# Fourth unit of the second MLP's down-projection in seven block products, and a later place for the last norm's transposes

## Chip, cores and metric

The kernel runs on one core of one Trainium2 chip. The metric is the device time of one execution in microseconds (us); for the kernel before, the median of three runs is 1207.76 us (1206.56 to 1208.12).

## What is computed

The reference is a trunk of two decoder layers on 512 tokens of width 1024, all in float32. Layer 0 mixes tokens by sliding-window attention beside a short convolution, layer 1 by gated linear attention. Each layer then has a gated MLP with a width-3 convolution, and a gated per-layer embedding. What the change touches is the end of layer 1:

```python
def _conv_ffn(h, w_up, conv_w, conv_b, w_down):
    u = _causal_depthwise_conv(h @ w_up, conv_w) + conv_b
    gate, up = jnp.split(u, 2, axis=-1)
    return (jax.nn.gelu(gate, approximate=False) * up) @ w_down      # w_down: 2816 x 1024
...
x = x + _conv_ffn(...)
gate = jax.nn.sigmoid(_rms_norm(x, norm) @ w_gate)                    # w_gate: 1024 x 1024
x = x + gate * (p_i @ w_proj)                                         # w_proj: 256 x 1024
```

## The kernel before, in words

**Layout.** The residual x is kept transposed as eight tiles `xT[m]` of 128 features x 512 tokens. A float32 product is made of three matmuls in a rounded type: each operand is split into a high part (a rounded copy, made by ScalarE) and a low part (the rest, a subtraction on VectorE), and the matmuls are high x high, high x low and low x high (`mm3`, lines 162 to 164; `cut` at 142 and 143 splits weights; `split` at 109 and 110 splits activations).

**Down-projection (`down`, from line 1088).** The 2816 rows of the weight are 22 blocks of 128, in three groups: B (0 to 7), A (8 to 13) and C (14 to 21). The 1024 output features are four *units* of 256, so a unit fills two PSUM banks. `plan` lists the steps in the order in which TensorE takes them: unit, row group, first and last block of the group, and as a fifth entry the unit whose block products are woven into this step. Inside `down` TensorE's order is written out by hand (`manual_schedule` at 1188); the other engines are ordered by a scheduler, which prefers what comes earlier in the program. Two such stages run, one per layer.

**Seven block products (`seven`, from line 857).** Group C of a unit is 8 row blocks x 256 features x 512 tokens. Taken as 2 x 2 blocks (even and odd row blocks, left and right features, left and right tokens) it is computed by seven products in place of eight. Each product is four row pairs x three matmuls, 256 tokens wide (lines 872 to 874). It needs sums and differences of weight blocks (`first_forms`, `more_forms`, `cut_blocks`, lines 811 to 855) and of activation blocks (`split_blocks`, 1006). The activation forms (`down_forms`) are made once per stage and lie in tiles with the tag b in the second MLP. In the first MLP all four units are computed this way; in the second MLP units 0, 1 and 2 are, and unit 3's group C is taken in two plain steps of four row blocks (`(3,"C",0,4)`, `(3,"C",4,8)`).

**After a unit.** `add` (line 1181) adds a unit's two banks to `xT`. Once `block_left` is 0, `finish` is called for the units that are complete. In the second MLP `finish` is `blocks` (line 287): gain, split, sums and differences for the block products of the next stage, and a square that is added up in the tile `self.acc` (line 285). Its scratch halves come from `both` (tag zt, two buffers), as do the weights that `load_inner` brings (line 1132); its results lie in tiles with the tags b (features 0 to 3) and a (4 to 7). The low and high parts of the activations of group B lie in tiles with tag a until their last use.

**Last stage (`ple1`, from line 1323).** The gate of layer 1, also by block products, with the weight as the moving operand. From line 1432 on TensorE, VectorE and ScalarE all take their instructions in program order. `add(X, "e1", ...)` is 24 matmuls into two banks X; the first two of eight steps of "s1" follow (six matmuls); then `end_norm` (line 322) transposes `self.acc` on TensorE (line 329), sums it on VectorE (331) and takes the root on GpSimd (172), which gives `self.r`. Then come two copies `ka` of X (line 1442), the split of `wt2` (line 1443), `load_p` (1444: eight transposes of p at line 1275 and their splits), the other six steps of "s1", and "s2" with `wt2` into X (line 1452). `self.r` is first read at line 1463. These are the lines on which the buffers of this place hang:

```python
self.acc = self.sp.tile([P, S], F32, tag="acc", name=self.nm("acc"), bufs=1)                      # 261
...
ka = [self.sp.tile([P, S], F32, tag="acc", name=self.nm("keep"), bufs=1), self.sq()]              # 1440
for k, x in zip(ka, X):
    nc.scalar.copy(k, x)
```

A tile whose tag has one buffer is written only once the instructions that use the earlier tile of that tag are done.

Of the kernel before, what the change touches and what calls it, by code (L numbers as in the profile page):

```python
# [56 lines left out]
class Kernel:  # L57
# [1030 lines left out]
    def down(self, i, acts, forms, both, work, finish):  # L1088


        nc, tc = self.nc, self.tc
        H = S // 2
        wd = self.a["ffn_w_down"][i].rearrange("(k p) n -> p k n", p=P)
        rows = {"A": (8, 14), "B": (0, 8), "C": (14, 22)}

        plan = [(0, "B", 0, 4), (0, "B", 4, 8), (0, "A", 0, 3), (0, "A", 3, 6)]
        plan += [(1, "A", 0, 3), (1, "A", 3, 6), (1, "B", 0, 4), (1, "B", 4, 8, 0)]
        plan += [(2, "B", 0, 4, 1), (2, "B", 4, 8, 2)]
        if i == 0:
            plan += [(2, "A", 0, 4, 3), (2, "A", 4, 6), (3, "B", 0, 4), (3, "B", 4, 8), (3, "A", 0, 3), (3, "A", 3, 6)]  # L1100
            loads = ["B0", "A0", "A1", "B1", "C0", "B2", "C2", "A2", "B3", "A3"]
            inner = ["C1", "C3"]
        else:
            plan += [(2, "A", 0, 3), (2, "A", 3, 6), (3, "B", 0, 4), (3, "B", 4, 8)]
            plan += [(3, "C", 0, 4), (3, "C", 4, 8), (3, "A", 0, 3), (3, "A", 3, 6)]
            loads = ["B0", "A0", "A1", "B1", "C0", "B2", "C2", "A2", "B3", "C3", "A3"]
            inner = ["C1"]
        blocked = 4 - i
        plan = [p if len(p) == 5 else p + (None,) for p in plan]
        got, cuts, gens, pending = {}, {}, {}, []  # L1110

        def pend():
            while pending:
                pending.pop(0)()

        def cols(u):
            return slice(2 * P * u, 2 * P * u + 2 * P)

        def load(key):
            k0, k1 = rows[key[0]]  # L1120
            u = int(key[1])
            raw = self.raw(k1 - k0, 2 * P)
            nc.sync.dma_start(raw, wd[:, k0:k1, cols(u)])
            got[key] = (raw, None)

        def load_inner(key):
            k0, k1 = rows[key[0]]
            u = int(key[1])
            parts = []
            for q in range(2):  # L1130
                t = both().rearrange("p a (b n) -> p (a b) n", n=2 * P)
                nc.sync.dma_start(t, wd[:, k0 + q : k1 : 2, cols(u)])
                parts.append(t)
            got[key] = (None, parts)

        def cut(t):
            u, name, k0, k1, _ = plan[t]
            cuts[t] = self.cut(got[f"{name}{u}"][0][:, k0:k1], "a")
            if k1 == rows[name][1] - rows[name][0] and loads:
                load(loads.pop(0))  # L1140

        def first_forms(u):
            raw, parts = got[f"C{u}"]
            ev, od = parts or self.by_parity(raw)
            gens[u] = ev, od, self.first_forms(ev, od, raw)

        def more_forms(u):
            ev, od, plain = gens[u]
            t13 = self.cut_blocks(ev)

            def rest():
                gens[u] = self.seven(od, (plain, t13, self.more_forms(ev, od)), acts[14:], forms, False)

            pending.append(rest)

        def cut_done(u):

            raw, _ = got[f"C{u}"]
            if raw is not None and loads:
                load(loads.pop(0))  # L1160
            elif raw is None and inner:
                load_inner(inner.pop(0))

        todo = []
        for t, p in enumerate(plan):
            todo.append((1, lambda t=t: cut(t)))
            if p[4] is not None:
                todo.append((1, lambda u=p[4]: first_forms(u)))
                todo.append((1, lambda u=p[4]: more_forms(u)))
        free = 3  # L1170

        def pump(n):
            nonlocal free
            free += n
            while todo and todo[0][0] <= free:
                need, f = todo.pop(0)
                free -= need
                f()

        def add(m, ps):  # L1180
            nc.vector.tensor_tensor(self.xT[m], self.xT[m], ps, ALU.add)

        due = [2 if u < blocked else 1 for u in range(4)]
        block_left = blocked
        next_unit = 0

        banks = {}
        with tc.manual_schedule(engines={ET.PE}):
            with tc.high_priority(offset=300):
                for _ in range(2):  # L1190
                    load(loads.pop(0))
                pump(0)
            for t, (u, name, k0, k1, s) in enumerate(plan):
                own = u not in banks
                if own:
                    banks[u] = [self.ps(), self.ps()]
                ends = t + 1 == len(plan) or plan[t + 1][0] != u
                joined = i == 0 and u == 3

                def steps(lo, hi):  # L1200
                    for k in range(lo, hi):
                        for c in range(2):
                            self.mm3(
                                banks[u][c], cuts[t](k, c * P, (c + 1) * P), acts[rows[name][0] + k0 + k],
                                start=own and k == 0, stop=ends and k == k1 - k0 - 1, skip_group_check=joined,
                            )

                def settled(ends):
                    nonlocal next_unit
                    if ends:  # L1210
                        for c in range(2):
                            add(2 * u + c, banks[u][c])
                        due[u] -= 1
                    while not block_left and next_unit < 4 and not due[next_unit]:
                        for m in (2 * next_unit, 2 * next_unit + 1):
                            finish(m)
                        next_unit += 1

                if s is None:
                    steps(0, k1 - k0)  # L1220
                    settled(ends)
                    pump(1)
                    pend()
                    if work:
                        work.pop(0)()
                        if not work:
                            load_inner(inner.pop(0))
                else:
                    g = gens[s]
                    steps(0, 1)  # L1230
                    next(g)
                    steps(1, 2)
                    next(g)
                    steps(2, 3)
                    next(g)
                    cut_done(s)
                    pump(1)
                    steps(3, 4)
                    pump(1)
                    settled(ends)  # L1240
                    X, Y, V = next(g)
                    pump(1)
                    x = self.xT[2 * s + 1].rearrange("p (u t) -> p u t", u=2)
                    nc.vector.tensor_tensor(x, x, V.unsqueeze(1).to_broadcast([P, 2, H]), ALU.add)
                    if i == 0 and s == 3:
                        banks[3] = [X, Y]
                    else:
                        add(2 * s, X)
                        add(2 * s + 1, Y)
                    pend()  # L1250
                    due[s] -= 1
                    block_left -= 1
                    settled(False)
# [69 lines left out]
    def ple1(self, fp):  # L1323
# [31 lines left out]
        def minus(out, x, y, parts=(0, 1)):  # L1355
            for q in parts:
                c = slice(2 * q, 2 * q + 2)
                nc.vector.tensor_tensor(out[:, c, :], x[:, c, :], y[:, c, :], ALU.subtract)
# [73 lines left out]
        with tc.manual_schedule(engines={ET.PE, ET.DVE, ET.Activation}):  # L1432
# [2 lines left out]
            minus(b11, b22, b11)  # L1435
            steps = [(j, i, both, Q[i]) for j in range(J) for i in range(2)]
            add(None, "s1", wt1, first=True, order=steps[:2])

            self.end_norm()
            ka = [self.sp.tile([P, S], F32, tag="acc", name=self.nm("keep"), bufs=1), self.sq()]  # L1440
            for k, x in zip(ka, X):
                nc.scalar.copy(k, x)
            wt2 = chunks(b11)
            pT = self.load_p(1, fp, pin)
            add(None, "s1", wt1, order=steps[2:])
            minus(b12, b22, b12, (0,))
            wj = chunk(wj_raw[:, 2:, :])
            kd = keep(Q, "R")
# [522 lines left out]
```

## Time and profile before

| | |
|---|---|
| median of three runs | 1207.76 us |
| profiled execution, its own time | 1206.43 us |
| its span from first to last instruction | 1204.7 us |
| TensorE busy, share of the span | 1197.7 us, 99% |
| VectorE / ScalarE busy | 968.3 us, 80% / 665.3 us, 55% |
| down-projection of the first MLP | from 409.44 to 525.41 us |
| down-projection of the second MLP | from 1029.19 to 1146.20 us |
| last stage | from 1146.20 us to the end |

In the lists of the trace each row begins with the start of an instruction and its duration, both in us, then engine, line, operation, output and inputs, and the shape. TensorE is pipelined: its durations overlap, so what one matmul costs is read from the distance of two starts. PEld is the load of a matmul's stationary operand.

### The profile page before, as it was taken

The numbers are of one execution on the slowest core, as the hardware profiler recorded it, in microseconds if no ns is written. First come the engines' busy times: TensorE is split into PE (matmuls) and PEld (weight loads), VectorE is DVE, ScalarE is ACT, GpSimd is POOL, SyncE is SP. The second block draws the span as 40 slices with busy tenths as digits, with TensorE's granted clock in tenths as the row PEclk, the third lists the DMA queues.
The fourth block names the chain that finished last, engine by engine and source line by source line (L and its number), as shares of the span: only waits on it lengthen the run. The fifth ranks groups of instructions, "written<-read, shape, count | busy, mean of one in ns | idle before, by whom it ended". The sixth has DMA issues, their size and how long they took to land.

```text
span 1204.7 us, 17692 instructions
## 1 busy us (share of the span) xinstructions
PE 1197.7 (99%) x7013; PEld 1036.9 (86%) x7013; DVE 968.3 (80%) x1527; ACT 665.3 (55%) x1081; POOL 43.8 (4%) x64
## 2 busy tenths in 40 slices
PE   9999999999999999999999999999999999999998
PEld 8877788999899889888988988889998899888887
DVE  6786587899998986746579876677999999988595
ACT  7466455656555644534573564555565645646374
POOL 2600000000000000000100000000000000000000
PEclk9999999999999999999999999999999999999999
DMA  7321322423333242222322222313242423322501
GB/s 222 93 85 45 96 74 70 140 71 108 103 106 104 91 137 97 96 89 94 115 93 68 73 70 71 105 49 127 70 141 70 136 75 120 134 88 97 210 1 70
DMA packets 111127, 117.61 MB, mean 98 GB/s; under 512 B 2840, under 2 KB 106322, under 8 KB 111044
## 3 DMA queue, kind: packets, MB, share of 16 engines
q1 hardware_dynamic: 109680, 115.35, 29.2%
q8 instruction: 55, 0.90, 0.3%
q0 software_dynamic: 560, 0.42, 0.3%
q10 hardware_dynamic: 804, 0.70, 0.2%
q14 instruction: 28, 0.23, 0.1%
HBM read 114.37 MB, written 2.10 MB: 97 GB/s over the span
## 4 chain that ended last, share of the span: by engine, by line
PE 87%; DVE 8%; ACT 2%; issue 1%; POOL 1%; DMA 0%; ACTq 0%; DVEq 0%; POOLq 0%
PE ps L162 12%; PE ps L163 12%; PE ps L164 12%; PE pa L163 7%; PE pa L162 7%; PE pa L164 7%; PE ps L872 5%; PE ps L874 5%; PE ps L873 5%; PE pa L872 2%; PE pa L874 2%; PE pa L873 2%; DVE wl L143 2%; PE ps L1371 1%; PE ps L1369 1%
## 5 line engine op out<-in xcount | busy, mean ns | idle before, releaser
L142 ACT ACTIVATE wh<-raw 128x1024 fp32r<-128x1024 f32 (+4 forms) x154 | 152.4, 991 | 155.1 <-PE ps L163 109.4
L143 DVE TENSOR_TENSOR wl<-raw,wh 128x1024 fp32r<-128x1024 f32 (+4 forms) x154 | 175.6, 1142 | 50.1 <-ACT wh L142 49.7
L819 ACT ACTIVATE wh<-raw 128x1024 fp32r<-128x1024 f32 x78 | 82.8, 1061 | 118.4 <-DVE raw L844 65.2
L932 DVE SCALAR_TENSOR_TENSOR zt<-z,vfa,zt 128x510 f32<-128x510 f32 (+1 forms) x176 | 130.6, 744 | 11.7 <-ACT zt L930 11.2
L820 DVE TENSOR_TENSOR wl<-raw,wh 128x1024 fp32r<-128x1024 f32 x78 | 95.3, 1222 | 19.3 <-ACT wh L819 19.2
L930 ACT ACTIVATE zt<-z,vfb 128x512 f32<-128x512 f32 x88 | 71.1, 810 | 28.9 <-DVE four L983 12.8
L162 PE MATMUL ps<-b,wh 128*128 128x512 f32 x192 | 76.8, 400 | 0.0
L163 PE MATMUL ps<-b,wh 128*128 128x512 f32 x192 | 75.1, 391 | 0.0
L164 PE MATMUL ps<-b,wl 128*128 128x512 f32 x192 | 75.0, 391 | 0.0
L163 PE MATMUL pa<-b,wh 128*128 128x512 f32 x176 | 69.0, 392 | 0.0
L163 PE MATMUL pa<-a,wh 128*128 128x512 f32 x176 | 69.0, 392 | 0.0
L162 PE MATMUL pa<-a,wh 128*128 128x512 f32 x176 | 69.0, 392 | 0.0
L162 PE MATMUL pa<-b,wh 128*128 128x512 f32 x176 | 69.0, 392 | 0.0
L164 PE MATMUL pa<-a,wl 128*128 128x512 f32 x176 | 68.4, 389 | 0.0
L164 PE MATMUL pa<-b,wl 128*128 128x512 f32 x176 | 68.4, 389 | 0.0
L872 PE MATMUL ps<-four,wh 128*128 128x256 f32 x232 | 65.1, 281 | 0.5 <-ACT ps L893 0.5
L874 PE MATMUL ps<-four,wl 128*128 128x256 f32 x232 | 64.4, 278 | 0.0
L873 PE MATMUL ps<-four,wh 128*128 128x256 f32 x232 | 64.2, 277 | 0.0
L162 PE MATMUL ps<-a,wh 128*128 128x512 f32 x160 | 63.1, 394 | 0.0
L163 PE MATMUL ps<-a,wh 128*128 128x512 f32 x160 | 62.6, 392 | 0.0
L164 PE MATMUL ps<-a,wl 128*128 128x512 f32 x160 | 62.5, 391 | 0.0
L162 PE MATMUL ps<-uh,wh 128*128 128x512 f32 x128 | 50.3, 393 | 0.0
(475 smaller groups left out, 3491.5 us busy)
## 6 DMA issues: line engine op xcount, KB each, us to landing
raw<-in_ffn_w_up_dram SPq DMA_DIRECT2D x44, 1024.0 KB, 5.0
raw<-in_ffn_w_down_dram SPq DMA_DIRECT2D x13, 1024.0 KB, 4.8
raw<-in_hy_w_in_dram SPq DMA_DIRECT2D x8, 1024.0 KB, 5.1
raw<-in_gla_w_in_dram SPq DMA_DIRECT2D x8, 1024.0 KB, 5.1
raw<-in_ffn_w_down_dram SPq DMA_DIRECT2D x8, 768.0 KB, 4.1
raw<-in_ple_w_gate_dram SPq DMA_DIRECT2D x6, 1024.0 KB, 4.8
raw<-in_hy_w_out_dram SPq DMA_DIRECT2D x16, 256.0 KB, 4.2
raw<-in_gla_w_out_dram SPq DMA_DIRECT2D x4, 1024.0 KB, 4.8
```

The lines of the kernel that those rows point to most:

```text
L142: nc.scalar.activation(hv, v, AF.Copy)
L143: nc.vector.tensor_tensor(lv, v, hv.bitcast(F32), ALU.subtract)
L162: mm(out, lh, rh, start=start, stop=False, **kw)
L163: mm(out, lh, rl, start=False, stop=False, **kw)
L164: mm(out, ll, rh, start=False, stop=stop, **kw)
L819: nc.scalar.activation(h, src, AF.Copy)
L820: nc.vector.tensor_tensor(l, src, h.bitcast(F32), ALU.subtract)
L872: mm(out, wh, xh, start=first and j == 0, stop=False, **kw)
L873: mm(out, wh, xl, start=False, stop=False, **kw)
L874: mm(out, wl, xh, start=False, stop=j == ND // 2 - 1, **kw)
L930: nc.scalar.activation(y, z, AF.Identity, scale=w2[:, f : f + 1], bias=bb[:, f : f + 1])
L932: nc.vector.scalar_tensor_tensor(out=y[:, tap:], in0=z[:, : S - tap], scalar=w[:, f : f + 1], in1=y[:, tap:], op0=ALU.mult, op1=ALU.add,)
```

## The change

Unit 3 of the second MLP gets the plan that the first MLP has: its group C is woven as seven block products into the first step of group A of unit 2, its weights come by `load_inner` into the zt buffers, and it accumulates into the same two banks as the plain steps of unit 3 (`joined`). With four blocks, `finish` begins after the fourth. In `ple1`, `end_norm` moves behind `load_p` and behind the other six steps of "s1"; the copies `ka`, `wt2` and `load_p` now stand ahead of it.

```diff
-        if i == 0:
-            plan += [(2, "A", 0, 4, 3), (2, "A", 4, 6), (3, "B", 0, 4), (3, "B", 4, 8), (3, "A", 0, 3), (3, "A", 3, 6)]
-            loads = ["B0", "A0", "A1", "B1", "C0", "B2", "C2", "A2", "B3", "A3"]
-            inner = ["C1", "C3"]
-        else:
-            plan += [(2, "A", 0, 3), (2, "A", 3, 6), (3, "B", 0, 4), (3, "B", 4, 8)]
-            plan += [(3, "C", 0, 4), (3, "C", 4, 8), (3, "A", 0, 3), (3, "A", 3, 6)]
-            loads = ["B0", "A0", "A1", "B1", "C0", "B2", "C2", "A2", "B3", "C3", "A3"]
-            inner = ["C1"]
-        blocked = 4 - i
+        plan += [(2, "A", 0, 4, 3), (2, "A", 4, 6), (3, "B", 0, 4), (3, "B", 4, 8), (3, "A", 0, 3), (3, "A", 3, 6)]
+        loads = ["B0", "A0", "A1", "B1", "C0", "B2", "C2", "A2", "B3", "A3"]
+        inner = ["C1", "C3"]
+        blocked = 4
...
-                joined = i == 0 and u == 3
+                joined = u == 3
...
-                    if i == 0 and s == 3:
+                    if s == 3:
                         banks[3] = [X, Y]
...
             add(None, "s1", wt1, first=True, order=steps[:2])
-
-            self.end_norm()
             ka = [self.sp.tile([P, S], F32, tag="acc", name=self.nm("keep"), bufs=1), self.sq()]
             for k, x in zip(ka, X):
                 nc.scalar.copy(k, x)
             wt2 = chunks(b11)
             pT = self.load_p(1, fp, pin)
             add(None, "s1", wt1, order=steps[2:])
+            self.end_norm()
             minus(b12, b22, b12, (0,))
```

## Prediction

> **What bounds the kernel now.** I read the page first, then who waited for whom, the two down-projections side by side by windows, and the last stage as a list in order of time.
>
> ```profile
> span 1204.7 us, 17692 instructions
> PE 1197.7 (99%) x7013; PEld 1036.9 (86%) x7013; DVE 968.3 (80%) x1527; ACT 665.3 (55%) x1081; POOL 43.8 (4%) x64
> ...
> PE pa L198 <- DVE mhalf L186: 1.3, 1, 1.3
> PE ps L872 <- ACT ps L893: 0.5, 2, 0.3
> ```
>
> TensorE is busy for 99% of the span, and of its waits in the whole trace the longest is 1.3 us, at the very start. A kernel in this state becomes shorter only by fewer matmul columns, and longer by any wait that reaches TensorE. So I ask of each edit two things: how many columns it takes away, and whether it makes TensorE wait.
>
> ```profile
> 409.44:525.41 115.97, 115.97 (x674) 101.25 (x673) 86.69 (x119) 55.06 (x80) 0.00 (x0) 1.00 0.29 97
> 1029.19:1146.20 117.01, 117.01 (x638) 100.56 (x637) 90.83 (x131) 58.32 (x85) 0.00 (x0) 1.00 0.39 133
> 1107.80:1125.00 17.20, 17.20 (x80) 14.29 (x79) 15.28 (x26) 10.77 (x17) 0.00 (x0) 1.00 0.32 108
> 1125.00:1146.20 21.20, 21.20 (x95) 17.54 (x94) 8.12 (x9) 4.36 (x6) 0.00 (x0) 1.00 0.73 261
> 1146.20:1158.43 12.23, 12.23 (x62) 10.28 (x60) 12.20 (x20) 9.99 (x17) 1.16 (x1) 1.00 0.00 1
> ```
>
> The columns are: stretch and its length, then busy time and count of PE, PEld, DVE, ACT and POOL, then granted clock (1.00 is full), DMA share, GB/s. The first two rows are the same stage in the two MLPs, the first with four units by block products, the second with three. The rest is the end of the second one, and the first 12.23 us of the last stage, in which VectorE has 12.20 us of work.
>
> **Part 1, the fourth unit: fewer columns.** Group C of unit 3 now takes 8 row blocks x 2 feature halves x 3 = 48 matmuls of 512 columns; as block products it takes 7 x 4 x 3 = 84 of 256. What one costs is the distance of two starts:
>
> ```profile
> 1040.10 0.39 PE L162 MATMUL ps<-four,wh 128*128 128x512 f32 x1
> 1044.86 0.39 PE L162 MATMUL ps<-four,wh 128*128 128x512 f32 x1
> ...
> 1016.86 0.28 PE L872 MATMUL ps<-b,wh 128*128 128x256 f32 x1
> 1019.47 0.28 PE L874 MATMUL ps<-four,sq 128*128 128x256 f32 x1
> ```
>
> The first two are 21 matmuls apart: 4.76/21 = 0.2267 us. The other two are 23 apart: 2.61/23 = 0.1135 us. So 84 x 0.1135 - 48 x 0.2267 = 9.53 - 10.88 = -1.35 us. The first MLP already runs the new plan, though, and there the stage takes 115.97 us against 117.01, which is -1.04 us: changes of width and waits for bank copies eat 0.3. I take -1.04, the row of the same code, and keep -1.35 as the lower end. For the upper end I take -0.7, should that loss of 0.3 come once more in the new place.
>
> The Trainium skill (TensorE: Matmul & The Clock Gate, section Back-to-back issue gap) speaks against this part: it gives a sustained spacing of about 81 ns for 128 columns and 131 ns for 512, because each narrow matmul needs its own weight load. A straight line between them, an estimate from that page, is 98 ns at 256, and the part would then cost 84 x 98 - 48 x 131 = +1.9 us. The two pitches above, 0.1135 and 0.2267 us, do not agree with it: here half the width costs half the time, so the rule changes nothing in the sum.
>
> **Part 1, what moves beside it.** The extra weight forms follow the path that unit 1 takes here:
>
> ```profile
> 1077.89 0.68 DVE L844 TENSOR_TENSOR zt<-zt,zt 128x512 f32<-128x512 f32 x1
> 1079.77 1.23 DVE L820 TENSOR_TENSOR wl<-zt,wh 128x1024 fp32r<-128x1024 f32 x1
> 1085.88 0.36 ACT L893 COPY ps<-ps 128x256 f32<-128x256 f32 x1 [0.41 <-PE ps L874]
> ...
> 1117.35 1.23 DVE L143 TENSOR_TENSOR wl<-raw,wh 128x1024 fp32r<-128x1024 f32 x1 [0.18 <-ACT wh L142]
> ```
>
> VectorE gains two splits of 1024 elements and eight operations of 512 (two splits, two differences for the first forms, two more and a narrow split for the later ones, one addition to the residual), and loses the two 1024-element splits of the plain steps: 8 x 0.68 = +5.4 us. ScalarE gains three copies of 512 and four of 256, about 3.3 us. Neither sets the end as long as it stays off TensorE's waits. The first MLP has that load with no more waits than here. What it does not have is the heavier `finish` of the second one, and this moves: `finish` for features 0 to 5 now starts after the fourth block, and the a tiles of group B come free later. Of VectorE's 15.28 + 8.12 = 23.40 us behind 1107.80, two splits of 1.23 go; 20.9 us remain for the 2.7 + 10.9 + 8.2 = 21.8 us of TensorE work (16 row blocks x 6 x 0.2267) behind the fourth block. It just fits, so I cost it at nothing; without the fit it is the second rival.
>
> The DMAs stand in these rows, the first two from the first MLP, where unit 3's weights already come this way:
>
> ```profile
> 463.38 4.04 SPq L1132 DMA_DIRECT2D zt<-in_ffn_w_down_dram  x2
> ...
> 487.68 0.68 DVE L843 TENSOR_TENSOR zt<-zt 128x512 f32<-128x512 f32 x1
> ...
> 1127.13 0.37 SPq L1259 DMA_DIRECT2D pin<-in_p_dram  x1
> ...
> pin<-in_p_dram SPq DMA_DIRECT2D x2, 256.0 KB, 3.1
> ```
>
> One 1 MB load goes, two of 512 KB come, about 20 us ahead of their use (467 against 487). The second half of p is loaded when the last activation of group B gives its buffer free, now at 1127.13. Then that is 8 us before the stage ends, and p is needed 6.8 us into the last stage (1153.00 below): its 3.1 us of flight are hidden, even if loads queue behind it on SP. I cost the DMAs at nothing; without their cover the price would be those few us of flight.
>
> **Part 2, the moved transposes.** Here is the place now:
>
> ```profile
> 1146.20 0.39 PE L1369 MATMUL ps<-wh,b 128*128 128x512 f32 x1
> 1153.00 0.60 PE L329 MATMUL pa<-cf,acc 128*128 128x128 f32 x4
> 1153.44 1.04 PE L1275 MATMUL pa<-cf,pin 128*128 128x128 f32 x8
> 1154.23 0.48 PE L1369 MATMUL ps<-wh,b 128*128 128x512 f32 x1
> 1158.43 0.39 PE L1369 MATMUL ps<-four,b 128*128 128x512 f32 x1
> 1158.65 0.39 PE L1370 MATMUL ps<-four,b 128*128 128x512 f32 x1
> ...
> 1151.83 0.68 DVE L285 TENSOR_TENSOR acc<-acc,sq 128x512 f32<-128x512 f32 x1
> 1157.03 2.35 DVE L1349 TENSOR_TENSOR four<-raw,four 128x1024 fp32r<-128x1024 f32 x2
> ...
> 1152.88 0.63 ACT L109 ACTIVATE a<-zt 128x512 fp32r<-128x512 f32 x1 [0.30 <-DVE zt L312]
> 1153.64 0.59 ACT L1442 COPY keep<-ps 128x512 f32<-128x512 f32 x1
> 1154.12 0.59 ACT L1442 COPY sq<-ps 128x512 f32<-128x512 f32 x1
> 1154.61 1.06 ACT L1348 ACTIVATE four<-raw 128x1024 fp32r<-128x1024 f32 x1
> ```
>
> What it removes: the sum of squares is complete at 1151.83 + 0.68 = 1152.51, the transposes start at 1153.00. TensorE does not wait for it now, so the move saves nothing in this trace; it only gives 5 us more room.
>
> What it adds: the first copy `ka` writes the one buffer of tag acc, in which the sum of squares lies. It starts at 1153.64, 0.04 us after the last transpose ended (1153.00 + 0.60), although the bank that it copies was complete 2.5 us earlier (1150.73 + 0.39, a row further down), and ScalarE's previous instruction ended at 1153.51. That is this buffer being handed over. The copy stays where it is in ScalarE's order, but the transposes go behind `load_p` and 18 matmuls. ScalarE takes its instructions in order, so behind the waiting copy stand the other copy, both splits of `wt2`, the splits of p, `wj` and the copies of Q; for `wt2` TensorE waits.
>
> The chain, on this trace's clock: the transposes would start where "s2" starts now, less the 0.44 us that they leave behind (1153.44 - 1153.00), so at 1158.43 - 0.44 = 1157.99, and end at 1158.59. Copies at 1158.63 and 1159.11; the first split of `wt2` at 1159.60, done at 1160.66; its low part on VectorE, one of the two in the row of 2.35, 1.2 us, done at about 1161.91. The first matmul of "s2" needs the high part (1160.7), the second the low part: it starts at about 1161.95 in place of 1158.65. That is +3.30 us on TensorE.
>
> Does it come back? Behind this point TensorE has no wait to swallow it, and "s2" is the only consumer that is late: the second split of `wt2`, p and `wj` follow at 1.1 us a split, ahead of the matmuls that need them. The root (`self.r`) comes some 8 us later than now and is read late:
>
> ```profile
> 1157.27 1.85 POOL L172 TENSOR_TENSOR rtok<-rs,mhalf 128x4 f32<-128x4 f32 x1 [339.85 <-DVE rs L171]
> ...
> 1173.64 0.21 ACT L1463 ACTIVATE rlo<-rtok 128x4 f32<-128x4 f32 x1
> ```
>
> It is written at 1159.12 now and about 1167 then, and read after 1173. No row here shows the wait of a copy on transposes that stand behind it, so its bounds are 0 (if the copy is not held) and 3.30 plus one more split, 4.5 us. I take 3.30, since the 0.04 us at 1153.64 is the nearest row.
>
> **Sum.** Against the profiled execution: 1206.43 - 1.04 + 3.30 = 1208.69 us. That execution is 1.33 us under the median of the runs, so on the scale of the runs 1207.76 + 2.26 = 1210.0 us, 0.19% above before. A change of 0.2% (2.4 us) is about what a measurement of this kernel can tell from none; my forecast lies just inside.
>
> **The rivals.**
>
> *The copy is not held, or its hold is covered* (1206.7 us). For it: 0.04 us is one event, and ScalarE was busy until 0.13 us before it. Then part 1 stands alone: 1207.76 - 1.04. Against it: the two tiles share one buffer, and a copy ahead of the transposes would destroy what they read. Chance 0.13.
>
> *VectorE is late at the end of the stage* (1212.2 us, slower). The place is the last pair of `finish` ahead of the stage's end. In the last stage the 21st matmul needs the low part of feature block 6:
>
> ```profile
> 1149.28 0.42 DVE L110 TENSOR_TENSOR a<-zt,a 128x256 fp32r<-128x256 f32 x1
> ...
> 1150.73 0.39 PE L1371 MATMUL ps<-wh,a 128*128 128x512 f32 x1
> ...
> 1123.93 1.89 DVE L110 TENSOR_TENSOR a<-zt,a 128x512 fp32r<-128x512 f32 x3
> ```
>
> It is ready at 1149.70 and used at 1150.73: 1.03 us of room, in a stretch where VectorE has no idle time (12.20 of 12.23). If the three low parts of the pair before (1.89) and its two squares (2 x 0.68) slip past the stage's end, VectorE is 3.25 us late and TensorE waits 2.2 us, on top of the forecast. It decides from 1.03 us of backlog on. For it: 20.9 of 21.8 us. Against it: much of that can run earlier, and splits of weights come first in the scheduler's order. Chance 0.12.
>
> *The clock drops after the new gap* (1212.7 us). TensorE would stand still for about 2.1 us, do one matmul, and wait 1.0 us more.
>
> ```profile
> 0.00:10.00 10.00, 8.68 (x43) 7.35 (x44) 3.28 (x8) 4.44 (x7) 0.34 (x6) 1.00 0.82 265
> ```
>
> The granted clock stays at 1.00 in the stretch that holds the longest gap of this trace, the 1.3 us at the start; a longer one is not in it. At half the clock, 12 matmuls of "s2" would take 2.7 us more. The Trainium skill (TensorE: Matmul & The Clock Gate, section What's actually happening) halves the clock after an idle window of about 3.4 us; no gap of this trace comes near that. Chance 0.05.
>
> **How the numbers follow.** Forecast 0.70, rivals 0.13, 0.12 and 0.05. The forecast's own range is 1208.9 to 1211.2: part 1 between -1.35 and -0.7, and the runs scatter by up to 1.2 us about their median, of which I take 0.8. The whole range takes in the first rival, the stall's upper bound and the second rival: 1205.9 to 1212.4. Within 0.2% means up to 1210.18: somewhat over half of the forecast (0.38) and nearly all of the first rival (0.11), so 0.49. Slower: the rest of the forecast (0.32) and the other two (0.12 and 0.05), so 0.49. Faster by over 0.2% needs more than the columns give: 0.02, out of the first rival.
>
> **What would show it.** In the profile after: 84 matmuls of 256 columns in place of 48 of 512, and a second down-projection of about 116 us. The copy at line 1442 starting within 0.1 us of the last transpose at line 329, with ScalarE idle for some 5 us ahead of it. A gap of 2 us ahead of the first matmul of "s2", and one of 1 us behind it. Wrong is the forecast if ScalarE runs the copy ahead of the transposes, if the down-projection does not fall by 0.5 to 1.35 us, or if TensorE waits ahead of "s1".

## The result, and the profile after

The changed kernel takes 1210.97 us (median of 6 runs, 1209.54 to 1212.49) against 1206.91 us for the kernel before (6 runs on the same chip, 1206.55 to 1208.12). The ratio is 1.0032, with a 95% interval of 1.0022 to 1.0042: slower by about 4 us. The forecast was +2.26 us; the time lies inside the range and the sign is right. Part of that is luck: the forecast added its 2.26 us to a median of 1207.76 us, and six runs put the kernel before at 1206.91, 0.85 us lower. The difference of 4.06 us is more than the largest that the forecast allowed itself without a rival (1211.2 - 1207.76 = 3.4 us).

The profiled execution took 1209.54 us, the fastest of the six. Its page begins:

```profile
span 1207.8 us, 17782 instructions
...
PE 1197.7 (99%) x7049; PEld 1037.2 (86%) x7049; DVE 972.3 (81%) x1535; ACT 668.0 (55%) x1088; POOL 43.9 (4%) x64
```

TensorE runs 36 matmuls more (7049 against 7013, which is 84 - 48). That its busy time is the same 1197.7 us says little about the columns: by windows it falls by 1.03 us in the down-projection and rises by 0.74 us in the last stage, where the matmuls are the same, and by 0.29 us ahead of both. A matmul that starts behind a wait is recorded longer (0.49 or 0.50 us in place of 0.39 in the list below). So the parts are read from the distance of starts.

Lines of the changed kernel stand six lower from 1175 to 1410 and eight lower in the last stage from 1432 on: the copies `ka` are L1434, `mm3` in `add` is L1363 to L1365, `chunk` is L1342 and L1343. The stages by windows, with the columns of before (the first MLP's down-projection, the second one's, and the last stage up to the transposes):

```profile
410.00:525.98 115.98, 115.98 (x674) 101.22 (x673) 86.70 (x119) 55.07 (x80) 0.00 (x0) 1.00 0.30 97
1029.76:1145.74 115.98, 115.98 (x675) 101.23 (x674) 93.97 (x138) 61.18 (x91) 0.00 (x0) 1.00 0.41 134
1145.74:1157.69 11.95, 11.95 (x58) 9.64 (x56) 11.09 (x17) 6.37 (x10) 0.00 (x0) 1.00 0.00 0
```

The second down-projection now takes 115.98 us, as the first does. That is 1.03 us less than before (117.01), and nothing in it waits. The loss is behind it. TensorE's list in order of time, around the moved transposes:

```profile
1145.74 0.39 PE L1363 MATMUL ps<-wh,b 128*128 128x512 f32 x1
...
1149.83 0.50 PE L1363 MATMUL ps<-wh,a 128*128 128x512 f32 x1
...
1150.40 0.40 PE L1365 MATMUL ps<-wh,a 128*128 128x512 f32 x1
...
1157.69 0.60 PE L329 MATMUL pa<-cf,acc 128*128 128x128 f32 x4
1160.40 0.49 PE L1363 MATMUL ps<-four,b 128*128 128x512 f32 x1 [2.12 <-ACT four L1342]
1161.66 0.50 PE L1364 MATMUL ps<-four,b 128*128 128x512 f32 x1 [0.77 <-DVE four L1343]
```

The brackets hold the idle time ahead of an instruction and what ended it. The second matmul of "s2" starts 15.92 us behind the start of the stage (1161.66 - 1145.74); before, it was 12.45 us (1158.65 - 1146.20). TensorE is 3.47 us later there, and 3.30 of them are the two gaps: from the transposes to the first matmul of "s2" 2.71 us pass, and 0.44 would do; from the first to the second 1.26 us, and 0.23 would do. The rest arose ahead of the transposes (11.95 us into the stage, where 12.23 - 0.44 = 11.79 would do). ScalarE shows where the gaps come from:

```profile
1152.81 0.63 ACT L109 ACTIVATE a<-zt 128x512 fp32r<-128x512 f32 x1 [0.30 <-DVE zt L312]
1158.32 0.59 ACT L1434 COPY keep<-ps 128x512 f32<-128x512 f32 x1 [4.88 <-PE pa L329]
1158.81 0.59 ACT L1434 COPY sq<-ps 128x512 f32<-128x512 f32 x1
1159.28 2.01 ACT L1342 ACTIVATE four<-raw 128x1024 fp32r<-128x1024 f32 x2
```

It stands idle for 4.88 us ahead of the first copy, released by the transposes, and begins 0.03 us after their end (1157.69 + 0.60 = 1158.29). Only then come the splits of `wt2` that TensorE needs. And VectorE:

```profile
1149.81 0.43 DVE L110 TENSOR_TENSOR a<-zt,a 128x256 fp32r<-128x256 f32 x1
...
1153.30 0.68 DVE L285 TENSOR_TENSOR acc<-acc,sq 128x512 f32<-128x512 f32 x1
...
1160.38 2.36 DVE L1343 TENSOR_TENSOR four<-raw,four 128x1024 fp32r<-128x1024 f32 x2 [3.53 <-ACT four L1342]
```

Its work is later than before, measured from the start of the stage: the sum of squares is complete at 8.24 us (1153.30 + 0.68 - 1145.74), against 6.31 us (1152.51 - 1146.20). The narrow low part is ready at 1150.24 and used at 1150.40: of 1.03 us of room, 0.16 is left. That use is itself 0.13 us later in the stage than before (4.66 us behind its start, against 4.53), since two matmuls earlier the high part of the same block (feature block 6) is only just in time (ready at 1149.37 + 0.40 = 1149.77, used at 1149.83).

The accounts of one execution each, from start to start of a stage's first and last matmul:

| | down-projection | last stage |
|---|---|---|
| before | 117.01 | 53.95 |
| changed | 115.98 | 57.58 |
| changed, again | 115.96 | 59.28 |
| new plan alone | 115.98 | 56.15 |
| move alone | 117.00 | 60.28 |

The profiled execution's +3.1 us are -1.03 in the down-projection, +3.63 in the last stage, and +0.57 that it was late already at the start of the down-projection (1029.76 against 1029.19, without a change there), less 0.07 behind the last matmul.

### The profile page after: what moved, and what is told of

The parts are those of the page before. It is cut to its first block, busy times and chain, and to the rows that moved or that the text cites. A ratio compares the mean times of both kernels' runs of the same rounds, so it can differ in the third digit from the quotient of the medians.

```text
span 1207.8 us, 17782 instructions
## 1 busy us (share of the span) xinstructions
PE 1197.7 (99%) x7049; PEld 1037.2 (86%) x7049; DVE 972.3 (81%) x1535; ACT 668.0 (55%) x1088; POOL 43.9 (4%) x64
## 4 chain that ended last, share of the span: by engine, by line
PE 79%; DVE 14%; ACT 3%; issue 2%; DMA 1%; POOL 1%; ACTq 0%; DVEq 0%; POOLq 0%
PE ps L162 12%; PE ps L163 12%; PE ps L164 12%; PE pa L163 5%; PE pa L162 5%; PE pa L164 5%; PE ps L872 5%; PE ps L874 5%; PE ps L873 4%; DVE zt L932 2%; DVE wl L143 2%; PE pa L872 2%; PE pa L874 2%; PE pa L873 2%; DVE wl L820 1%
## 5 line engine op out<-in xcount | busy, mean ns | idle before, releaser
L872 PE MATMUL ps<-four,wh 128*128 128x256 f32 x240 | 67.4, 281 | 0.7 <-ACT ps L893 0.5
L873 PE MATMUL ps<-four,wh 128*128 128x256 f32 x240 | 66.4, 277 | 0.0
```

What stands on the lines that cost most here:

```text
L872: mm(out, wh, xh, start=first and j == 0, stop=False, **kw)
L873: mm(out, wh, xl, start=False, stop=False, **kw)
```

## The experiments

Each kernel is the changed one with an edit; where only the move is kept, it is the kernel before with an edit. Theory A: only the copy that waits for the buffer of tag acc holds ScalarE, and with it TensorE. Theory B: VectorE's backlog counts too. Theory C: the gap costs clock besides. "Before" is the kernel before in the same set of runs.

**New plan alone** (`end_norm` back in its old place).

```diff
+            self.end_norm()
             ka = [...]
...
             add(None, "s1", wt1, order=steps[2:])
-            self.end_norm()
```

> Part 1 alone: the new plan, the norm's transposes at their old place, ahead of the copies. Theory A (the loss is ScalarE held by the copy that waits for the moved transposes): the down-projection keeps its -1.03 us, and now the transposes wait for the sum of squares: it is complete at 1153.98 in the changed kernel, 8.24 us after the stage begins, and the transposes' old place is 6.80 us behind it, so TensorE waits about 1.4 us there; in all about +0.4 us against before, and no wait at s2. Theory B (the loss comes from VectorE's backlog at the end of the down-projection): the loss stays without the move, +3 us or more.

Measured: 1207.51 us (1206.97 to 1210.21, 11 runs), before 1207.14; ratio 1.0005 [0.9996, 1.0014]. The down-projection has its full gain and the last stage eats it, by TensorE's waits:

```profile
PE pa L329 <- DVE acc L285: 1.2, 1, 1.2
PE ps L1363 <- ACT a L109: 0.5, 1, 0.5
```

In the old place the transposes now wait 1.2 us for the sum of squares, and a high part of `finish` is 0.5 us late. A is right in the sum (+0.4 us) and in the wait at the transposes. B as it was recorded, +3 us or more without the move, is wrong, but the 0.5 us are its kind of loss: the new plan takes back through VectorE what it gains on TensorE. Its slowest execution, 1210.21 us, shows a mean granted clock of 0.998, without the gaps of the changed kernel.

**Move alone** (the old plan, the new place of `end_norm`). The edit is the diff of the front, its first part undone.

> Part 2 alone: the plan of before, the norm's transposes behind the other six steps of s1. Theory A: the wait at s2 is all there, +3.3 to +3.6 us against before. Theory B: no difference, since the plan is the old one. Theory C (beside A, the gap of 2 us also costs clock in most executions, and that is why the median rose by 4.1 us and the profiled execution by 3.1): +4 us or more, with a granted clock under 1.0 in several executions.

Measured: 1211.60 us (1210.01 to 1212.92, 5 runs), before 1207.14; ratio 1.0036 [1.0023, 1.0048]. The gaps are there without the new plan, so the move makes them. But +4.5 us is more than A's 3.3 to 3.6. TensorE's list and the windows of the profiled execution (the slowest of the five; L1369 to L1371 are `mm3` here):

```profile
1160.87 0.49 PE L1369 MATMUL ps<-four,b 128*128 128x512 f32 x1 [2.12 <-ACT four L1348]
1162.13 0.79 PE L1370 MATMUL ps<-four,b 128*128 128x512 f32 x1 [0.77 <-DVE four L1349]
...
1163.14 0.63 PE L1369 MATMUL ps<-four,b 128*128 128x512 f32 x1
1163.57 0.63 PE L1370 MATMUL ps<-four,b 128*128 128x512 f32 x1
...
1166.98 1.65 PE L1377 MATMUL pa<-cf,xT 128*128 128x128 f32 x8
```

```profile
1161.00:1162.00 1.00, 0.36 (x1) 0.05 (x1) 1.00 (x2) 1.00 (x2) 0.00 (x0) 0.71 0.00 0
1162.00:1163.00 1.00, 0.87 (x2) 0.78 (x3) 1.00 (x2) 1.00 (x3) 0.00 (x0) 0.50 0.00 0
...
1168.00:1169.00 1.00, 1.00 (x8) 0.92 (x7) 1.00 (x2) 0.87 (x2) 0.00 (x0) 0.88 0.00 0
```

The gaps are the changed kernel's, 2.12 and 0.77 us. From within the second gap on the granted clock, the eighth number, is 0.50 for about 6.8 us (from 0.58 us before 1162.00, by the mean of 0.71, to 0.24 us behind 1168.00, by that of 0.88), and a matmul takes 0.43 us in place of 0.2267. From 1162.13 to 1166.98 there are 11 of them: 4.85 us, where the changed kernel's trace has 2.63 (1161.66 to 1164.29). The eight transposes behind them take 1.41 us (1166.98 to 1168.39) in place of 0.79 there. That is 2.8 us lost; the whole last stage is 2.70 us longer than in that trace (60.28 against 57.58).

**Both parts, the copy into another buffer** (the acc buffer goes to a copy later in the stage).

```diff
-            ka = [self.sp.tile(..., tag="acc", bufs=1), self.sq()]
+            ka = [result(), self.sq()]
...
-            kb = [self.sq(), result()]
+            kb = [self.sq(), self.sp.tile(..., tag="acc", bufs=1)]
```

> Both parts, but the first copy of X lies in one of the three z buffers and the second copy after s2 takes the acc buffer, so nothing waits for the transposes. Theory A: the gaps ahead of s2 are gone, and the down-projection's gain is left, -1.0 us against before, about 1205.9 us. Theory B: still slower than before by about 3 us. Theory C: as A, and the scatter of the executions shrinks to that of before.

Measured: 1206.44 us (1205.70 to 1210.63, 11 runs), before 1207.14; ratio 0.9997 [0.9988, 1.0006]. One name of a buffer gives back the stall: -0.7 us against before, where the changed kernel had +4.1. The transposes stay in their late place, and the copy begins as soon as ScalarE comes to it:

```profile
1152.50 0.56 ACT L1434 COPY so<-ps 128x512 f32<-128x512 f32 x1
```

A's -1.0 us is not all there. One wait is left in the profile, at the high part of feature block 6 in "e1":

```profile
PE ps L1363 <- ACT a L109: 0.6, 1, 0.6
```

Nor did the scatter shrink as C expected: one of the eleven executions took 1210.63 us, at a mean clock of 0.998.

**Both parts, the copies behind the splits** (the two copies moved down in ScalarE's order, still into the acc buffer).

```diff
-            for k, x in zip(ka, X):
-                nc.scalar.copy(k, x)
             wt2 = chunks(b11)
             pT = self.load_p(1, fp, pin)
+            for k, x in zip(ka, X):
+                nc.scalar.copy(k, x)
```

> Both parts, with the two copies still in the acc buffer and still held, but moved behind the splits of wt2 and of p in ScalarE's order. Theory A: only the copies themselves are late; s2 waits for one copy behind the transposes, about 0.9 us, and the sum is about -0.1 us against before. If the wait came from the transposes themselves and not from what stands behind the copy, it stays at about 3 us and the sum at +2 to +3.

Measured: 1207.56 us (1206.78 to 1208.71, 11 runs), before 1207.14; ratio 1.0005 [0.9996, 1.0014]. The copies still wait for the transposes, but `wt2` no longer stands behind them. TensorE's waits:

```profile
PE ps L1363 <- ACT keep L1436: 1.1, 1, 1.1
PE ps L1363 <- ACT a L109: 0.4, 1, 0.4
```

The first is the write of "s2" into the banks that `ka` must copy first. The second is the wait in "e1" again; its 0.4 us are about what lies between A's -0.1 us and the measured +0.4. Together with the kernel above this shows A's chain: the buffer holds the copy, and program order passes that hold on.

**Move alone, other buffer** (the move alone, with the buffers swapped as above).

> The plan of before, the norm's transposes moved, and the first copy of X in a z buffer (the second copy after s2 takes the acc buffer). Theory A (ScalarE held by the copy that waits for the acc buffer): the move by itself costs nothing, 0 against before, about 1207.1 us. If the move itself costs (its place between s1 and s2, the later root), +3 us or more is left, as in the run with the move alone.

Measured: 1207.15 us (1206.45 to 1208.56, 11 runs), before 1206.97; ratio 1.0003 [0.9994, 1.0012]. No wait of TensorE is left in the stage. The late place by itself costs nothing.

**The gap filled** (the changed kernel with 13 idle matmuls behind the transposes, which no result uses).

```diff
             self.end_norm()
+            spare = self.pa()
+            for n in range(13):
+                nc.tensor.matmul(spare, self.ones_r, ..., start=True, stop=True)
```

> The changed kernel, with 13 more matmuls of 512 columns behind the transposes, into a bank that nobody reads: 13 x 0.227 = 2.95 us of work in the 3.1 us in which TensorE stands still. The wait for ScalarE is the same. Theory A alone: no difference to the changed kernel, about 1211.0 us. Theory C (the gap also costs clock in most executions): the median falls to what the profiled execution shows, 1209.5 to 1210.2 us, and no execution has a clock under 0.999.

Measured: 1210.03 us (1208.77 to 1210.87, 9 runs), before 1206.97; ratio 1.0027 [1.0017, 1.0036]. That is +3.1 us against before, where the changed kernel had +4.1, and no execution has a clock under 0.999, as C expected. The two were not measured in one set, so they were both run again (below).

**The gap longer** (five more copies ahead of `wt2`).

```diff
-            for k, x in zip(ka, X):
+            for k, x in list(zip(ka, X)) + 5 * [(ka[1], X[1])]:
```

> The changed kernel with five more copies of 512 columns on ScalarE behind the two held ones: ScalarE gains 5 x 0.48 = 2.4 us in the chain ahead of s2, and TensorE's gap grows from 2.1 to about 4.5 us. Theory A alone: +2.4 us against the changed kernel, about 1213.4 us, clock 1.0. Theory C: the clock now drops to a half in every execution, as it did in the profiled execution with the move alone (for 6.7 us there, 3.4 us lost): about 1216.8 us and a clock of 0.996 to 0.997.

Measured: 1214.29 us (1213.15 to 1215.90, 5 runs), before 1206.97; ratio 1.0064 [1.0051, 1.0077]: above A, below C. The mean granted clock is 0.996 or 0.997 in all five; the kernel before never shows less than 0.999. TensorE's first matmuls of "s2", and the windows:

```profile
1162.75 0.79 PE L1363 MATMUL ps<-four,b 128*128 128x512 f32 x1 [5.20 <-ACT four L1342]
1164.01 0.79 PE L1364 MATMUL ps<-four,b 128*128 128x512 f32 x1 [0.47 <-DVE four L1343]
```

```profile
1159.00:1160.00 1.00, 0.00 (x0) 0.00 (x0) 0.00 (x0) 0.94 (x3) 0.00 (x0) 0.98 0.00 0
1160.00:1161.00 1.00, 0.00 (x0) 0.00 (x0) 0.00 (x0) 0.97 (x2) 0.00 (x0) 0.50 0.00 0
...
1166.00:1167.00 1.00, 1.00 (x5) 0.76 (x4) 0.97 (x4) 0.52 (x2) 0.00 (x0) 0.61 0.00 0
```

The clock fell inside the gap, 2.4 us after it began (at 1159.96 by the mean of 0.98 in the window from 1159.00; the gap began at 1157.55), and came back about 4 us after TensorE's work began again. The last stage is 4.27 us longer than in the first profile of the changed kernel (61.85 against 57.58). Of these the two gaps are 5.20 + 0.47 - 2.12 - 0.77 = 2.78, which leaves about 1.5 us for the clock: for much of the time at half clock TensorE had nothing to do. C's 3.4 us counted all of that time as work.

**The changed kernel again, and the gap filled again** (both unaltered, on one chip).

> The changed kernel unaltered, on one chip with the next run. In its profiled execution the parts are -1.03 us in the down-projection and +3.6 us in the last stage; its first six executions had a median of +4.1 us against before. If the 1.0 us between them is lost clock behind the gap in part of the executions, the median stays near +4 us, and the executions spread over 1209.5 to 1212.5 us. If it was chance, the median comes to +2.5 to +3.2 us.

> The changed kernel with 13 idle matmuls in the gap, on the same chip as the run before this one. If the gap costs clock, about 1 us below it (1210.0 us), as the first time; if not, the same as it within 0.3 us.

Measured: 1211.15 us (1210.62 to 1212.66, 5 runs) and 1209.56 us (1209.07 to 1211.11, 11 runs), before 1207.29; ratios 1.0038 [1.0026, 1.0051] and 1.0021 [1.0012, 1.0030]. The kernel with 13 matmuls more is 1.6 us faster. The clocks of the unfilled one's five runs are 0.999, 0.998, 0.996, 0.996, 0.999, and its two slowest are those at 0.996; the filled one has 1.000 in all eleven. The filling leaves the stall as it was: from the transposes to the second matmul of "s2" it takes 3.98 us (1157.42 to 1161.40), in both profiles of the changed kernel 3.97. What it removes is TensorE's idle time:

```profile
1157.42 0.60 PE L329 MATMUL pa<-cf,acc 128*128 128x128 f32 x4
1157.77 3.24 PE L1441 MATMUL pa<-ones_r 128*128 128x512 f32 x13
1160.85 0.39 PE L1363 MATMUL ps<-four,b 128*128 128x512 f32 x1
1161.40 0.50 PE L1364 MATMUL ps<-four,b 128*128 128x512 f32 x1 [0.16 <-DVE four L1343]
```

The profiled execution of the changed kernel, by windows and TensorE's list:

```profile
1161.00:1162.00 1.00, 0.87 (x3) 0.73 (x4) 1.00 (x2) 1.00 (x3) 0.00 (x0) 0.78 0.00 0
1162.00:1163.00 1.00, 1.00 (x4) 0.80 (x3) 1.00 (x3) 1.00 (x2) 0.00 (x0) 0.50 0.06 16
...
1164.00:1165.00 1.00, 1.00 (x4) 0.81 (x3) 0.96 (x3) 0.00 (x0) 0.64 (x1) 0.51 0.00 0
1165.00:1166.00 1.00, 1.00 (x8) 0.86 (x8) 1.00 (x2) 0.62 (x1) 1.00 (x1) 1.00 0.00 0
```

```profile
1161.47 0.54 PE L1365 MATMUL ps<-four,b 128*128 128x512 f32 x1
...
1165.12 0.40 PE L1365 MATMUL ps<-four,b 128*128 128x512 f32 x1
```

These two rows are nine matmuls apart: 3.65 - 9 x 0.2267 = 1.6 us lost to the clock, and its last stage is 1.70 us longer than in the first profile of the same kernel (59.28 against 57.58), where the clock is 1.00 throughout. C is shown: it happens in some executions and not in others. A mean clock of 0.999 alone does not tell the two apart: the last kernel below has it in its profile too, where the clock falls only in the last 2.3 us, when TensorE has no work left (0.54 and 0.50 in the windows behind 1202.00).

**Other buffer, and the last weight splits first** (the swapped buffers, and a higher priority in the scheduler for the splits of the last two weight pieces).

```diff
-            cuts[t] = self.cut(...)
+            with tc.high_priority(offset=60) if i == 1 and t + 2 >= len(plan) else ExitStack():
+                cuts[t] = self.cut(...)
```

> Both parts with the copies in swapped buffers, and besides the weight splits of the last two plain steps (group A of unit 3) ahead of the block sums in VectorE's order. In the run without this TensorE waits 0.6 us in e1 for a high part of feature block 7 that is late because b12 is loaded late, because the low part of the last weight split came 3.5 us behind its high part on VectorE. If that chain is what eats the rest of part 1's gain: no wait in e1, -1.0 to -1.3 us against before, about 1206.0 us. If not: as the run without it, 1206.4 us.

Measured: 1205.94 us (1205.38 to 1207.96, 11 runs), before 1206.97; ratio 0.9993 [0.9984, 1.0002]. Run once more, unaltered:

> The version with swapped buffers and the splits ahead, again: -1.0 us against before, as the first time; with two series the interval should leave out 1.0.

Measured: 1206.09 us (1205.04 to 1206.55, 11 runs), before 1207.29; ratio 0.9991 [0.9982, 1.0000]. TensorE has no wait left in the stage in either profile, and the medians are 1.0 and 1.2 us under before, but each interval still reaches 1.0.

**New plan alone, the last weight splits first** (the old place of `end_norm`, with the priority).

> Part 1 alone, the norm's transposes at their old place, and the weight splits of the last two plain steps ahead in VectorE's order. If the late weight split (through the late load of b12) is what makes the sum of squares late, TensorE's two waits of the run with part 1 alone (1.2 us at the transposes, 0.5 us in e1) go, the move was not needed, and the sum is -1.0 us against before, about 1206.0 us. If the sum of squares is late for another reason (the block sums themselves), about 1 us at the transposes stays and the sum is 0.

Measured: 1206.15 us (1205.49 to 1207.07, 11 runs), before 1207.29; ratio 0.9989 [0.9980, 0.9998]: 1.1 us under before, and the interval leaves out 1.0. TensorE has no wait left in the stage. The chain of the last weight piece, first in the new plan alone, then here:

```profile
1134.27 1.88 DVE L110 TENSOR_TENSOR a<-zt,a 128x512 fp32r<-128x512 f32 x3
1136.07 0.95 DVE L143 TENSOR_TENSOR wl<-raw,wh 128x768 fp32r<-128x768 f32 x1
1137.08 0.37 SPq L1330 DMA_DIRECT2D raw<-in_ple_w_gate_dram  x1
1142.94 1.23 DVE L1352 TENSOR_TENSOR raw<-raw,raw 128x1024 f32<-128x1024 f32 x1 [3.43 <-DMA raw<-in_ple_w_gate_dram]
...
1153.56 0.68 DVE L285 TENSOR_TENSOR acc<-acc,sq 128x512 f32<-128x512 f32 x1
```

```profile
1134.15 0.95 DVE L143 TENSOR_TENSOR wl<-raw,wh 128x768 fp32r<-128x768 f32 x1
1135.13 0.37 SPq L1330 DMA_DIRECT2D raw<-in_ple_w_gate_dram  x1
1141.80 1.23 DVE L1352 TENSOR_TENSOR raw<-raw,raw 128x1024 f32<-128x1024 f32 x1 [1.73 <-DMA raw<-in_ple_w_gate_dram]
...
1151.57 0.68 DVE L285 TENSOR_TENSOR acc<-acc,sq 128x512 f32<-128x512 f32 x1
```

In the new plan alone the split stands behind three low parts of activations. The split gives its buffer free, the gate's weight is loaded into it, and VectorE waits for that load. The second kernel runs 0.56 us later here, and yet its load goes out 1.95 us earlier, and VectorE idles 1.7 us less. Measured from the start of the stage, the sum of squares is complete at 8.86 us in the first kernel and at 6.31 us in the second (1152.25 - 1145.94), as early as before the change.

## Why the prediction was right, and what it mis-sized

**Part 1, fewer columns: right.** -1.04 us was forecast from the first MLP's row and -1.03 measured; in every kernel with the new plan the stage took 115.89 to 116.00 us. It is the step from -1.35 to -1.04, by the first MLP's row, that made this exact. The +1.9 us that was worked out from the Trainium skill (TensorE: Matmul & The Clock Gate, section Back-to-back issue gap) is not there.

**Part 2, the held copy: right.** The stall was to be 3.30 us and is 3.30 by the distance of starts, in two gaps that were to be 2 and 1 us and are 2.12 and 0.77; the copy was to start within 0.1 us of the transposes and did within 0.03; ScalarE was to idle for some 5 us and did for 4.88. That it goes away with another buffer, with either plan, shows the cause. The first rival, a copy not held, is excluded by this.

**The clock, the third rival at 0.05: the main size that was off.** Forecast +2.26, measured +4.06; the sum had nothing for the clock. The clock is the largest part of the 1.8 us between them: it cost 1.6 us in one profile of the changed kernel, 2.7 us in one of the move alone, none in the other profile of the changed kernel, and filling the gap brought the median down by 1.6 us on one chip and by 1.0 us across two sets. The prediction's price of 2.7 us for half the clock was near; its chance was not. It took the clock for a rival to the stall, and it comes on top of the stall in part of the executions.

Its only row was a single gap of 1.3 us, which says nothing of two with one matmul between. The row is doubtful besides, by the same trace:

```profile
1.32 3.35 PE L198 MATMUL pa<-ones_r 128*128 128x512 f32 x7 [1.32 <-DVE mhalf L186]
4.47 1.06 PE L469 MATMUL ps<-cf,xin 128*128 128x128 f32 x4
```

Right behind that gap seven matmuls of 512 columns take 3.15 us, 0.45 us each, while the 13 idle ones of the same form took 0.24 us each (1157.77 to 1160.85). That is the pace of half the clock, in a window that shows 1.00. So this row could not vouch for a clock that stays up.

The Trainium skill (TensorE: Matmul & The Clock Gate, section What's actually happening) says that the gate falls to half after an idle window of about 3.4 us, and that the window runs freely, so that runs of one kernel differ. The traces agree with the length and with the free run: the clock stood at half for 3.4 us in the repeated run and for 6.8 us in the move alone and in the longer gap, once and twice that window. They do not agree with a wholly idle window, nor with 3.4 us as a bound on one gap: the clock fell 3.8 us after the first gap began in the repeated run (1157.75 to 1161.56), 2.7 us in the move alone (1158.75 to 1161.42), both with one matmul in between, and 2.4 us in the unbroken longer gap. In the 3.41 us just ahead of these falls TensorE was busy for 0.92, 1.23 and 0.99 us. An emptier stretch of that length did no harm in the first profile of the changed kernel:

```profile
1158.25:1161.66 3.41, 0.53 (x2) 0.19 (x1) 1.27 (x2) 3.34 (x5) 0.00 (x0) 1.00 0.00 0
```

So how empty a stretch is does not decide alone. That windows with fixed edges are counted, and that it depends on where the edges fall, would fit these four traces; no run here moves the edges, so it is not shown.

**"It just fits, so I cost it at nothing": failed by a little.** VectorE's busy time rose by 4.0 us where 5.4 were forecast, ScalarE's by 2.7 where 3.3 were. Not the sum failed; what failed is the step from "the work fits" to "its order holds". The prediction held against its second rival that splits of weights come first in the scheduler's order; the last one came behind three low parts of activations. The split that frees a buffer went late, so the load of the next weight went late, and VectorE waited for it. In the changed kernel this left 0.16 us of room; in the new plan alone it costs 0.5 us, at the high part of the feature block whose low part the second rival named. That wait comes and goes: it is in five of the eight profiles with the new plan and without the priority, 0.2 to 0.7 us long, and in none of the three with it. At 2.2 us the rival was not seen.

**"The move saves nothing in this trace": right of the trace, wrong of the kernel.** With the new plan the transposes would have waited in their old place (1.2 us in the new plan alone). The move removes that wait, and the buffer takes back nearly three times as much (3.30 us). The two parts were priced one by one on the old trace, and they meet. The priority shows that the wait could go without the move.

Open is which of two executions loses the clock. Nor is the clock the whole scatter: the slowest of the first six runs (1212.49 us) has a mean clock of 1.000, which leaves no room for 3.4 us at half (the repeated run's profile, with 3.4 us at half, has 0.999), and no trace shows what made it slow. The 0.57 us by which the first profile was late at the down-projection are there at the first MLP's already (410.00 against 409.44), in code that the change leaves alone; over all the profiles that stage of the second MLP starts between 1028.87 and 1030.17 us, so they are scatter.

## What to carry to other kernels

When a consumer is moved later, look up which buffer it reads and who writes that buffer next: the writer is held until then, and on an engine that works in program order so is everything behind it. When a part adds work to an engine that "just fits", ask not only for the sum but which of its instructions frees a buffer for a load, and put that one first. Price the second part of a change on the schedule that the first part makes, not on the old one.

## What was not expected of the hardware

TensorE's granted clock fell to 0.50 at two gaps of 2.12 and 0.77 us with one matmul between, for 3.4 us in one profile and 6.8 us in another, and not at all in a third. With a gap of 5.20 us the mean clock was 0.996 or 0.997 in all five executions; in the profiled one it fell 2.4 us into the gap. 13 idle matmuls in the gap made the kernel 1.6 us faster on the same chip, though they do nothing for the result.
